# A hybrid attention and recurrence layer: two block sizes per step in the recurrent heads, and four reordered queues

## The chip, the cores and the metric

The kernel runs on one core of a Trainium2 chip. The metric is the device time of one execution in microseconds (us). The core's engines work side by side, each through its own queue of instructions in order: PE (TensorE, matrix products; its weight loads are listed as PEld), DVE (VectorE), ACT (ScalarE), POOL (GpSimd) and SP (SyncE, which issues the DMA transfers). An instruction waits at the head of its queue until what it needs is there, and everything behind it waits too.

## The reference

One decoder layer on 1024 tokens of width 1024, in float32: a normalised input goes through one projection to an attention mixer (8 heads of 64) and to a gated recurrence (4 heads of 128); both results are projected back and added, and a feed-forward block with a squared ReLU follows. For each recurrent head, with f the forget gate of every channel:

```python
def hgrn2_recurrence(q, f_pre, i, gate, lower_bound, out_gain):
    """f = lb + (1-lb) sigmoid(f_pre); S_t = diag(f_t) S_{t-1} + (1-f_t) i_t^T;
    o_t = S_t^T q_t; y = RMSNorm_head(o) * silu(gate)."""
...
    h = rmsnorm(x, mix_pre_norm); proj = h @ w_in
    attn = rmsnorm(dilated_mixture_attention(q_a, k_a, v_a, slopes), attn_out_norm)
    rec = hgrn2_recurrence(q_h, f_h, i_h, g_h, lower_bounds, hgrn_out_norm)
    x = x + rmsnorm(concat([attn, rec]) @ w_out, mix_post_norm)
    ff = square(relu(rmsnorm(x, mlp_pre_norm) @ w_ff1)) @ w_ff2
    x = x + rmsnorm(ff, mlp_post_norm)
```

## The kernel before, in words

**Products.** A large matrix product is made from three products of the high and low parts of its operands (`three_pass`, L86 to L88). `split_into` makes the parts: ACT copies the source, rounded (L82), and VectorE subtracts that from it (L83). In the recurrent heads the products are plain F32. In the feed-forward block the products are recombined in seven per 2x2 blocks (`mm1` for the first matrix, `mm2` for the second).

**Order.** Everything is written out by hand; an engine takes its instructions in the order in which the program issues them. `fill(ns)` takes pieces of projection work off a list of generators until their counted costs (650 for three products of 512 columns, 330 for three of 256) come to `ns`. So the recurrent heads and the attention steps are written with fills between their own steps, and PE has projection products to do while VectorE works. `hgrn_ig` and `hgrn_qf` are such generators (the next head's projections), `attn_proj(pr)` makes an attention pair's queries, values and keys, and `drain` runs what is left.

**Start.** `keep_warm` (L278) issues products of a zero tile. Then the first token block is transposed (`x_turn`), one of eight 128-column pieces at a time, with a warm call between two, and the first weights are split (`w_split`). ACT and VectorE evacuate each transpose.

**A recurrent head.** The decays between a query and an earlier key inside a block of 128 tokens are products over ranges of tokens. `hgrn_core` (L371) builds the 128 x 128 score blocks `at` of the eight token blocks by seven levels, at block sizes c = 1, 2, 4 to 64 (L385). A level multiplies the keys with the second half of the queries of each pair of blocks (L392, eight products of 64 columns into one PSUM bank `pl`), then VectorE multiplies the first halves of the keys (L396) and the second halves of the queries (L398) by the block totals of the decay, makes the totals of twice the size (L402), and copies the level's scores into `at` where a mask says so (L403, a predicated copy). A fill of 2900 follows each level. Ahead of the levels stand a fill of 2200, the diagonal (`pd`, L377, from `prod`, L367), and a fill of 2300. After them `kt` is transposed (`pk`, L414; ACT copies it to `ktr`, L415), and the chunk states (`pu`, L422) and the outputs (`po`, L439, L441) follow. Four heads run one after the other, heads 0 to 2 beside the next head's projections and head 3, whose fills are scaled by 1.15, beside `attn_proj(0)`. The gates of a head are evacuated by `ig_evac`: ACT for the values `inat` (L229), VectorE for `gate` (L230).

**Attention.** 64 steps, each with scores (`ps`), transposes of the weights (`pt`) and sums over values, with fills between; `hooks` runs other work at given steps. `keys_off` (L469, L471) evacuates keys (`kf`, `kh`, `kl`) and copies them by DMA. `v_turn` transposes a pair's values in the middle of a later projection product.

**Output projection.** A loop over the eight token blocks t: `late_out` (products `pwo`), `row_turn` (transposes `pmt`), `residual`, `row_attn` (two VectorE operations that scale a later attention row, L702), `mixed_half`, `next_turn`, `residual_b`.

**Feed-forward.** The opening handles the first two column pairs of the first matrix apart, with the products in the order 1, 2, 3, 5, 6, 4, 7; `out_p5` (L1094), `out_p6` (L1097), `out_p7` and their like evacuate each product, `b_split` and `w1_split` split operands, `w1_load` loads raw pairs. Then `ff1(q)` runs over the other pairs. The second matrix runs over 49 units; behind unit 0 the last pair's activations are summed and stored (`act_sums`, `act_store`). At the end each token block gets its plain part (L1602 adds it), its norm and a gain (L1613).

```python
    for li, c in enumerate(LEVELS):
...
            for n in range(NT):
                TE.matmul(pl[:, n * 64:(n + 1) * 64], kt[:, n * P:(n + 1) * P],
                          qv[:, n * nb:(n + 1) * nb, 1, :], start=True, stop=True)
...
            fill(2900 * scale)
```

Of the kernel before, what the change touches and what calls it, by code (L numbers as in the profile page):

```python
# [17 lines left out]
P = 128  # L18
# [17 lines left out]
def hymba_layer(ctx, tc, x, w_in, w_out, w_ff1, w_ff2, g_pre, lb_logits, g_mix, g_post,  # L36
# [28 lines left out]
    masks = cp.tile([P, len(LEVELS), 64], U8, name="masks")  # L65
    gpre = cp.tile([P, NK], F32, name="gpre")
# [241 lines left out]
    V.tensor_copy(masks, mraw)  # L308
    V.tensor_tensor(out=lb, in0=lbl[:, :, 0], in1=lbl[:, :, 1], op=ALU.subtract)
# [14 lines left out]
    def hgrn_ig(h):  # L324
        hd = heads[h] = new_head(h)
        w_get(4 * h + 1)
        for t2 in range(NT // 2):
# [7 lines left out]
            ig_evac(hd, pm, (t2 * 2, t2 * 2 + 1))  # L335
# [34 lines left out]

    def hgrn_core(h, scale, after=None):  # L371
        hd = heads[h]
        inat, gate, prod, qt, kt, tot = (hd[n] for n in ("inat", "gate", "prod", "qt", "kt", "tot"))
        fill(2200 * scale)
# [8 lines left out]
        cur = tot  # L383
        fill(2300 * scale)
        for li, c in enumerate(LEVELS):  # L385
            nb = 64 // c
            qv = qt.rearrange("p (b two c) -> p b two c", two=2, c=c)
            kv = kt.rearrange("p (b two c) -> p b two c", two=2, c=c)
            av = at.rearrange("p n (b two c) -> p n b two c", two=2, c=c)
            pl = bank("s", f"pl{h}_{li}")  # L390
            for n in range(NT):
                TE.matmul(pl[:, n * 64:(n + 1) * 64], kt[:, n * P:(n + 1) * P],  # L392
                          qv[:, n * nb:(n + 1) * nb, 1, :], start=True, stop=True)
            w = T // (2 * c)
            cv = cur[:, :2 * w].rearrange("p (b two) -> p b two", two=2)
            V.tensor_tensor(out=kv[:, :, 0, :], in0=kv[:, :, 0, :],  # L396
                            in1=cv[:, :, 1:2].to_broadcast([P, w, c]), op=ALU.mult)
            V.tensor_tensor(out=qv[:, :, 1, :], in0=qv[:, :, 1, :],  # L398
                            in1=cv[:, :, 0:1].to_broadcast([P, w, c]), op=ALU.mult)
            nx = slab("P", f"tot{h}_{w}") if w > 64 else \  # L400
# [505 lines left out]
    for t in range(NT):  # L906
# [6 lines left out]
        if t > 0:  # L913
            residual(t - 1)
# [776 lines left out]
```

## Time and profile before

| | us |
|---|---|
| median of three runs (1299.04, 1296.51, 1299.54) | 1299.04 |
| profiled execution | 1296.25 |
| its span | 1294.4 |
| PE busy | 1254.5 (97%) |
| PEld busy | 1071.5 (83%) |
| DVE busy | 857.5 (66%) |
| ACT busy | 515.6 (40%) |
| POOL busy | 295.5 (23%) |

The recurrent heads take the span from about 60 to 320 us, attention goes on to about 600, the output projection to about 700, and the feed-forward block takes the rest. A row of the timeline has the start, the duration, the engine, the line, the operation, the tiles written and read, shapes, the count, and in brackets the idle time of the engine ahead of it and the engine and line that ended it. Successive PE products overlap, so the time that one costs is the distance from start to start and not its duration. The rows that matter stand in the prediction.

### The profile page before, as it was taken

What the parts mean: (1) busy time and instruction counts of PE and PEld (TensorE: products, weight loads), DVE (VectorE), ACT (ScalarE), POOL (GpSimd) and SP (SyncE); (2) the same over time, 40 slices, a digit from 0 to 9 for tenths busy, and PEclk for the clock granted to TensorE, in tenths of its full rate; (3) what the DMA queues carried; (4) which work ended last, traced back from release to release, by engine and by line L of the source; (5) the groups of instructions that cost most, each with busy time, mean ns of one, the idle gap of its engine ahead of it and who ended that gap; (6) DMA issues with size and microseconds to landing.
All of it is one profiled execution on the core that took longest, in us unless ns stands there. A gap on an engine that the chain in (4) does not pass through costs nothing. (4 is left out here: it accounts for less than half of the span.)

```text
span 1294.4 us, 17367 instructions
## 1 busy us (share of the span) xinstructions
PE 1254.5 (97%) x6666; PEld 1071.5 (83%) x6666; DVE 857.5 (66%) x1395; ACT 515.6 (40%) x904; POOL 295.5 (23%) x308
## 2 busy tenths in 40 slices
PE   8999999999999999899999899999999999999997
PEld 8898989988888887787877788888878888888885
DVE  5565656575665656667758566666675777688956
ACT  6612121222555555574655322222234633344412
POOL 0000000011112123134350387575541000000012
PEclk9999999999999999999999999999999999999998
DMA  5201111132223223326242345453478454434423
GB/s 204 66 17 51 33 44 38 29 86 66 82 66 82 66 82 80 127 70 221 97 148 90 138 171 179 147 179 127 142 260 333 163 195 130 156 105 131 156 75 126
DMA packets 58577, 153.98 MB, mean 119 GB/s; under 512 B 4992, under 2 KB 12928, under 8 KB 58240
## 3 DMA queue, kind: packets, MB, share of 16 engines
q1 hardware_dynamic: 58496, 152.89, 35.6%
q8 instruction: 52, 0.85, 0.3%
q14 instruction: 29, 0.24, 0.1%
HBM read 106.73 MB, written 39.85 MB: 113 GB/s over the span
## 5 line engine op out<-in xcount | busy, mean ns | idle before, releaser
L87 PE MATMUL f<-bl,ah 128*128 128x512 f32 x392 | 152.6, 389 | 0.5 <-DVE bl L83 0.5
L86 PE MATMUL f<-bh,ah 128*128 128x512 f32 x392 | 152.6, 389 | 0.0
L88 PE MATMUL f<-bh,al 128*128 128x512 f32 x392 | 152.5, 389 | 0.0
L83 DVE TENSOR_TENSOR al<-ar,ah 128x1024 fp32r<-128x1024 f32 x49 | 60.7, 1239 | 50.2 <-ACT ah L82 21.6
L87 PEld LDWEIGHTS f<-bl,ah 128*128 128x128 f32 x392 | 73.6, 188 | 16.1 <-DVE bl L83 0.8
L86 PEld LDWEIGHTS f<-bh,ah 128*128 128x128 f32 x392 | 73.6, 188 | 15.6 <-ACT acc L1471 0.4
L88 PEld LDWEIGHTS f<-bh,al 128*128 128x128 f32 x392 | 73.6, 188 | 15.1
L82 ACT ACTIVATE ah<-ar 128x1024 fp32r<-128x1024 f32 x49 | 52.3, 1067 | 53.6 <-DMA ar<-actd 28.2
L1607 POOL TENSOR_SCALAR fp<-fss 128x1 f32<-128x1 f32 x8 | 3.5, 432 | 268.3 <-ACT fd L1604 268.3
L576 DVE CUSTOM_DVE_ANT_0 p<-ps,bt 128x512 f32<-128x512 f32 (+2 forms) x84 | 44.3, 552 | 24.1 <-PE ps L574 23.9
L603 ACT ACTIVATE pth<-pt 128x512 fp32r<-128x512 f32 (+2 forms) x96 | 43.2, 486 | 41.1 <-PE pt L600 39.4
L604 DVE TENSOR_TENSOR ptl<-pt,pth 128x512 fp32r<-128x512 f32 (+2 forms) x96 | 50.2, 551 | 13.1 <-ACT pth L603 13.1
L392 PEld LDWEIGHTS pl<-qt,kt 128*128 128x128 f32 x448 | 53.7, 194 | 1.5 <-PE pm_av L88 0.9
L392 PE MATMUL pl<-qt,kt 128*128 128x64 f32 x448 | 53.8, 273 | 0.5 <-DVE qt L398 0.5
L587 ACT ACTIVATE p<-p,nm 128x128 f32<-128x128 f32 (+3 forms) x64 | 49.5, 773 | 9.2 <-DVE nm L582 6.2
L229 ACT ACTIVATE inat<-pig,rstd 128x128 f32<-128x128 f32 x32 | 11.6, 367 | 97.3 <-PE pig L88 84.2
L78 POOL TENSOR_SCALAR ms<-hss 128x8 f32<-128x8 f32 x4 | 0.8, 197 | 210.0 <-DVE hss L444 210.0
L82 ACT ACTIVATE bh<-br 128x1024 fp32r<-128x1024 f32 x28 | 29.9, 1068 | 42.6 <-PE f L88 37.3
L633 POOL TENSOR_TENSOR anat<-anat,rd 128x128 f32<-128x128 f32 x32 | 14.5, 455 | 140.4 <-DVE anat L632 136.6
L600 PE MATMUL pt<-ident,p 128*128 128x128 f32 x288 | 42.9, 276 | 3.4 <-DVE ptl L604 3.4
L1127 POOL TENSOR_TENSOR e<-x,e 128x512 f32<-128x512 f32 x14 | 20.7, 1476 | 102.0 <-DVE x L1078 102.0
L396 DVE TENSOR_TENSOR kt<-kt,tot 128x512 f32<-128x512 f32 x28 | 20.2, 722 | 35.8 <-PE pl L392 35.8
(1586 smaller groups left out, 3869.1 us busy)
## 6 DMA issues: line engine op xcount, KB each, us to landing
ar<-actd SPq DMA_DIRECT2D x49, 512.0 KB, 3.7
raw<-in_w_in_dram SPq DMA_DIRECT2D x28, 512.0 KB, 3.6
w1r<-in_w_ff_dram SPq DMA_DIRECT2D x14, 1024.0 KB, 6.5
br<-in_w_ff_dram SPq DMA_DIRECT2D x14, 1024.0 KB, 6.5
actd<-e SPq DMA_DIRECT2D x17, 768.0 KB, 4.3
actd<-e SPq DMA_DIRECT2D x11, 1024.0 KB, 4.1
xr<-in_x_dram SPq DMA_DIRECT2D x8, 512.0 KB, 8.7
raw<-in_w_out_dram SPq DMA_DIRECT2D x8, 512.0 KB, 3.7
```

The costliest lines, as they stand in the source:

```text
L82: S.activation(hi, src, AF.Copy)
L83: eng.tensor_tensor(out=lo, in0=src, in1=f32(hi), op=ALU.subtract)
L86: TE.matmul(dst, lhs[0], rhs[0], start=start, stop=False)
L87: TE.matmul(dst, lhs[0], rhs[1], start=False, stop=False)
L88: TE.matmul(dst, lhs[1], rhs[0], start=False, stop=stop)
L392: TE.matmul(pl[:, n * 64:(n + 1) * 64], kt[:, n * P:(n + 1) * P], qv[:, n * nb:(n + 1) * nb, 1, :], start=True, stop=True)
L576: V.tensor_tensor_reduce(out=pe[:, k0:k0 + n], in0=pS[:, :n], in1=bts[hd][:, o:o + n], scale=1.0, scalar=-3.0e38, op0=ALU.add, op1=ALU.max ...
L587: S.activation(pe[:, :nk], pe[:, :nk], AF.Exp, bias=nm[:, b:b + 1], accum_out=dn[:, b:b + 1])
L600: TE.transpose(pt[:, j * P:(j + 1) * P], pe[:, jj * P:(jj + 1) * P], ident)
L603: S.activation(hi, src, AF.Copy)
L604: V.tensor_tensor(out=lo, in0=src, in1=f32(hi), op=ALU.subtract)
L1127: eng[0].tensor_tensor(out=e1[:, 3], in0=a21, in1=e1[:, 2], op=ALU.add)
```

## The change

- **Recurrent heads.** The levels at c = 1 to 32 become three steps that each handle two block sizes, c and 2c with c = 1, 4, 16; c = 64 stays a level of its own. `quarter_sets` makes, for each half of the tokens, a set of 192 query columns per token block: the second halves at size c, and the last two quarters of each block of four, without and with the decay of the quarter between. A step makes eight products of 192 columns into four banks (tags s and t), and VectorE then updates queries, keys and totals in quarters and copies each bank into `at` in three predicated copies of 128 elements (12 per step; the third goes by the new masks `near`). The level at c = 64 is copied by ACT without a mask. Fills: 3300 ahead of the diagonal (2200), 1200 (2300), 7000 after each step, 3400 after the last level (2900 after each level).
- The gates of heads 1 to 3 are evacuated by ACT. The masks `near` are made from `masks` at the start.
- **First pair's values.** In `attn_proj(0)` both halves are transposed in the key products, the first in the first, the second in the second; before, the first one in the second value product and the second in the first key product.
- **Four queues.** At the start nine warm calls stand ahead of the transposes, none between, and five behind; the weight splits come earlier. `keys_off` runs behind a step's hooks. `row_attn` runs ahead of `residual`. In the feed-forward opening `out_p6` of each pair follows its part of the T3 split, the splits of pair 2 stand ahead of `out_p3` and `out_p7`, and pair 4 is loaded after them. The stores of the last pair's activations move from unit 0 to unit 2, and at the end the last block's gain is multiplied into both pieces after the second sum.

```diff
...
@@ -279,14 +280,12 @@
      groups = ((0, 1), (1, 1), (2, 2), (4, 2), (6, 1), (7, 1))
-    keep_warm(3)
+    keep_warm(9)
     for k in range(NK):
         x_turn(0, 1, k)
-        keep_warm(1)
-        if k == 3:
+        if k in (3, 4):
             w_split()
-    w_split()
-    keep_warm(2)
+    keep_warm(5)
     for i, grp in enumerate(groups):
         for k in range(NK):
             if i + 1 < len(groups):
@@ -297,8 +296,8 @@
...
         if i == 4:
+            ig_evac(heads[0], pms0[0], PAIRED[0])
             w_split()
-            ig_evac(heads[0], pms0[0], PAIRED[0])
             ig_evac(heads[0], pms0[1], PAIRED[1])
@@ -306,6 +305,11 @@
         ig_evac(heads[0], pms0[q], PAIRED[q])
     w_split()
     V.tensor_copy(masks, mraw)
+    first = col("lowhalf", 3)
+    V.tensor_reduce(first, mraw[:, 0:6].rearrange("p (s two) j -> p s two j", two=2)[:, :, 0], axis=AX.X, op=ALU.max)
+    V.tensor_scalar(first, first, -1.0, 1.0, op0=ALU.mult, op1=ALU.add)
+    V.tensor_tensor(out=near, in0=mraw[:, 0:6].rearrange("p (s two) j -> p s two j", two=2)[:, :, 1],
+                    in1=first.unsqueeze(2).to_broadcast([P, 3, 64]), op=ALU.mult)
...
@@ -332,7 +336,9 @@
                                k == 0, k == NK - 1)
                     if not (u == 1 and k == NK - 1):
                         yield 330.0
-            ig_evac(hd, pm, (t2 * 2, t2 * 2 + 1))
+            for u, t in enumerate((t2 * 2, t2 * 2 + 1)):
+                S.activation(hd["inat"][:, t], pm[:, u, 0], AF.Copy, scale=rstd0[:, t:t + 1])
+                S.activation(hd["gate"][:, t], pm[:, u, 1], AF.Copy, scale=rstd0[:, t:t + 1])
@@ -368,10 +374,35 @@
+    def quarter_sets(hd, h, step, tots):
+
+        c = 4 ** step
+        nb = 32 // c
+        qt = hd["qt"]
+        cv = tots.rearrange("p (n b f) -> p n b f", n=NT, f=4)
+        sets = []
+        for hf in range(2):
+            q = qt[:, hf * 512:hf * 512 + 512]
+            z = slab("T", f"qs{h}_{step}{hf}", F32, (P, 4, 192))
+            n4 = slice(hf * 4, hf * 4 + 4)
+            S.activation(z[:, :, :64].rearrange("p n (g c) -> p n g c", c=c),
+                         q.rearrange("p (n g two c) -> p n g two c", n=4, two=2, c=c)[:, :, :, 1], AF.Copy)
+            z2 = z[:, :, 64:128].rearrange("p n (b two c) -> p n b two c", two=2, c=c)
+            q4 = q.rearrange("p (n b f c) -> p n b f c", n=4, f=4, c=c)
+            S.activation(z2[:, :, :, 0], q4[:, :, :, 2], AF.Copy)
+            V.tensor_tensor(out=z2[:, :, :, 1], in0=q4[:, :, :, 3],
+                            in1=cv[:, n4, :, 2:3].to_broadcast([P, 4, nb, c]), op=ALU.mult)
+            V.tensor_tensor(out=z[:, :, 128:].rearrange("p n (b w) -> p n b w", b=nb),
+                            in0=z[:, :, 64:128].rearrange("p n (b w) -> p n b w", b=nb),
+                            in1=cv[:, n4, :, 1:2].to_broadcast([P, 4, nb, 2 * c]), op=ALU.mult)
+            sets.append(z)
+        return sets, cv
+
     def hgrn_core(h, scale, after=None):
         hd = heads[h]
         inat, gate, prod, qt, kt, tot = (hd[n] for n in ("inat", "gate", "prod", "qt", "kt", "tot"))
-        fill(2200 * scale)
+        ready = quarter_sets(hd, h, 0, tot)
+        fill(3300 * scale)
         pd = bank("t", f"pd{h}")
         for c in range(NT):
             TE.matmul(pd[:, c:c + 1], prod[:, c * P:(c + 1) * P], ones, start=True, stop=True)
@@ -380,32 +411,67 @@
         at = slab("S", f"at{h}", F32, (P, NT, P))
         V.tensor_tensor(out=at, in0=ident.unsqueeze(1).to_broadcast([P, NT, P]),
                         in1=dg.unsqueeze(2).to_broadcast([P, NT, P]), op=ALU.mult)
-        cur = tot
-        fill(2300 * scale)
-        for li, c in enumerate(LEVELS):
...
+        fill(1200 * scale)
+        totals = slab("P", f"tot{h}")
+        for step in range(3):
+            c = 4 ** step
+            nb = 32 // c
+            sets, cv = ready
+            banks4 = []
+            for u in range(4):
+                pl = bank("st"[u // 2], f"pl{h}_{step}{u}").rearrange("p (n q) -> p n q", n=2)
+                for n in range(2 * u, 2 * u + 2):
+                    TE.matmul(pl[:, n % 2, :192], kt[:, n * P:(n + 1) * P], sets[u // 2][:, n % 4],
+                              start=True, stop=True)
+                banks4.append(pl)
+            w = T // (4 * c)
+            at_ = (0, 768, 960)[step]
+            tots = totals[:, at_:at_ + 3 * w].rearrange("p (i w) -> p i w", i=3)
+            u23, u123, nx = (tots[:, i] for i in range(3))
+            cw = cv.rearrange("p n b f -> p (n b) f")
+            q4 = qt.rearrange("p (m f c) -> p m f c", f=4, c=c)
+            k4 = kt.rearrange("p (m f c) -> p m f c", f=4, c=c)
+
+            def spread(ap, k=c):
+                return ap.unsqueeze(2).to_broadcast([P, w, k])
+            V.tensor_tensor(out=q4[:, :, 1], in0=q4[:, :, 1], in1=spread(cw[:, :, 0]), op=ALU.mult)
+            for hf in range(2):
+                n4 = slice(hf * 4, hf * 4 + 4)
+                V.tensor_tensor(out=qt[:, hf * 512:hf * 512 + 512].rearrange("p (n b f c) -> p n b (f c)", n=4, f=4, c=c)
+                                [:, :, :, 2 * c:],
+                                in0=sets[hf][:, :, 128:].rearrange("p n (b w) -> p n b w", b=nb),
+                                in1=cv[:, n4, :, 0:1].to_broadcast([P, 4, nb, 2 * c]), op=ALU.mult)
+            V.tensor_tensor(out=u23, in0=cw[:, :, 2], in1=cw[:, :, 3], op=ALU.mult)
+            V.tensor_tensor(out=u123, in0=cw[:, :, 1], in1=u23, op=ALU.mult)
+            V.tensor_tensor(out=nx, in0=cw[:, :, 0], in1=u123, op=ALU.mult)
+            if step < 2:
+                ready = quarter_sets(hd, h, step + 1, nx)
+            V.tensor_tensor(out=k4[:, :, 2], in0=k4[:, :, 2], in1=spread(cw[:, :, 3]), op=ALU.mult)
+            V.tensor_tensor(out=k4[:, :, 1], in0=k4[:, :, 1], in1=spread(u23), op=ALU.mult)
+            V.tensor_tensor(out=k4[:, :, 0], in0=k4[:, :, 0], in1=spread(u123), op=ALU.mult)
+            for u, pl in enumerate(banks4):
+                for part_, mask, c2 in ((0, masks[:, 2 * step], c), (2, masks[:, 2 * step + 1], 2 * c),
+                                        (1, near[:, step], 2 * c)):
+                    av = at[:, 2 * u:2 * u + 2].rearrange("p n (b two c) -> p n b two c", two=2, c=c2)
+                    V.copy_predicated(
+                        av[:, :, :, 1, :],
+                        mask.rearrange("p (b c) -> p b c", c=c2).unsqueeze(1).to_broadcast([P, 2, 64 // c2, c2]),
+                        pl[:, :, part_ * 64:part_ * 64 + 64].rearrange("p n (b c) -> p n b c", c=c2))
             cur = nx
-            fill(2900 * scale)
+            fill((7000, 7000, 7000)[step] * scale)
+        pl = bank("s", f"pl{h}_6")
+        for n in range(NT):
+            TE.matmul(pl[:64, n * 64:(n + 1) * 64], kt[:, n * P:n * P + 64], qt[:, n * P + 64:(n + 1) * P],
+                      start=True, stop=True)
+        S.activation(at[:64, :, 64:], pl[:64].rearrange("p (n c) -> p n c", n=NT), AF.Copy)
+        kv, qv = (x.rearrange("p (n two c) -> p n two c", two=2, c=64) for x in (kt, qt))
+        cv = cur.rearrange("p (n two) -> p n two", two=2)
+        V.tensor_tensor(out=qv[:, :, 1], in0=qv[:, :, 1], in1=cv[:, :, 0:1].to_broadcast([P, NT, 64]), op=ALU.mult)
+        V.tensor_tensor(out=kv[:, :, 0], in0=kv[:, :, 0], in1=cv[:, :, 1:2].to_broadcast([P, NT, 64]), op=ALU.mult)
+        nx = tp.tile([P, NT], F32, tag="tot8", name=f"tot{h}_8", bufs=1)
+        V.tensor_tensor(out=nx, in0=cv[:, :, 0], in1=cv[:, :, 1], op=ALU.mult)
+        cur = nx
+        fill(3400 * scale)
         ktr = slab("T", f"ktr{h}", F32, (P, NT, P))
         for hf in range(2):
             pt = bank("t", f"pk{h}_{hf}")
@@ -495,7 +561,7 @@
             yield 650.0
         vs = slab("V8", f"v{pr}", F32R, (P, NT, 2, 2, 64))
-        late = None
+        late = []
 
         def v_turn(full, hf):
             pt = bank("mm", f"pvt{pr}{hf}")
@@ -510,13 +576,13 @@
             n = 0
             for cost in proj_t(w, f"av{pr}", hf, box):
                 n += 1
-                if n == 4 and late is not None:
-                    v_turn(*late)
+                if n == 4 and pr > 0 and late:
+                    v_turn(*late.pop(0))
                     cost += 450.0
                 yield cost
             full = half(f"vf{pr}{hf}")
             V.tensor_tensor(out=full, in0=box[0], in1=rrow[:, sl], op=ALU.mult)
-            late = (full, hf)
+            late.append((full, hf))
             yield 650.0
@@ -529,8 +595,8 @@
             n = 0
             for cost in proj_t(w, f"ak{pr}", hf, box):
                 n += 1
-                if n == 3 and hf == 0:
-                    v_turn(*late)
+                if n == 3 and late:
+                    v_turn(*late.pop(0))
                     cost += 450.0
                 yield cost
@@ -872,9 +938,6 @@
         if not fresh:
             look(s + 2)
         turn(hd, b, exped.pop(s))
-        if b in (7, 0, 1):
-            while put_off:
-                keys_off(*put_off.pop())
         if b % 2:
             to_weigh.append((hd, b // 2))
         to_fold, last_fold = [(i, g, weigh(i, g)) for i, g in ready], to_fold
@@ -888,6 +951,9 @@
         for i, g, a in last_fold:
             finish(i, g, *a)
         hooks.get(s, lambda: None)()
+        if b in (7, 0, 1):
+            while put_off:
+                keys_off(*put_off.pop())
         fill(3400.0 - 360.0 * b if s < n_steps - 20 else 1000.0 if s < n_steps - 16 else 1300.0)
         finish(i, g, *a)
@@ -910,10 +976,10 @@
             if t + 4 < NT:
                 row_load(t + 4)
+        if NE <= t + 2 < NT:
+            row_attn(t + 2)
         if t > 0:
             residual(t - 1)
-        if NE <= t + 2 < NT:
-            row_attn(t + 2)
...
@@ -1298,23 +1364,28 @@
     for q in range(2):
         mm1(q, 6, "b", True)
         w1_drop(q, "S")
-    b_split("T3", h11)
+    b_open("T3")
+    for c in range(2):
+        split_into(bops["T3"][2 * c], bops["T3"][2 * c + 1], h11[:, 2 * c:2 * c + 2])
+        out_p6(c)
     large.add("A")
-    for q in range(2):
-        out_p6(q)
     w1_sums(2, V)
     for q in range(2):
         mm1(q, 4, "d", False)
     wide_split(2)
+    wd = large.get("wd2", F32R)
+    split_into(wd[:, 0:2], wd[:, 2:4], w1raw[2][:, 2:4])
+    ops1[2]["D"] = wd
+    ops1[2][7], ops1[2][4] = halves_of((wd[:, 0:2], wd[:, 2:4]))
+    drop(w1raw.pop(2))
+    w1_load(4)
+    w1_split(2, 3)
     for q in range(2):
         out_p3(q)
     for q in range(2):
         mm1(q, 7, "b", False)
         w1_drop(q, "D")
         out_p7(q)
-    w1_split(2, 2)
-    w1_load(4)
-    w1_split(2, 3)
     act_plain(0)
     act_plain(1)
 
@@ -1573,6 +1644,7 @@
         drop(*aop.pop(n), *bop.pop(n))
         if n == 0:
             act_sums(NPAIR - 1)
+        if n == 2:
             act_store(NPAIR - 1)
         if h == nh - 1:
             for i in range(4):
@@ -1609,8 +1681,9 @@
                     end_out(*late)
                 if t < 2:
                     fold_in(7, 5, t)
-            if last:
-                V.tensor_tensor(out=c, in0=c, in1=gend[:, j], op=ALU.mult)
+            if last and j:
+                for i, e in enumerate(pieces):
+                    V.tensor_tensor(out=e, in0=e, in1=gend[:, i], op=ALU.mult)
...
```

More of the change, by code (lines that the diff above doesn't have):

```diff
@@ L382, in hgrn_core @@
                         in1=dg.unsqueeze(2).to_broadcast([P, NT, P]), op=ALU.mult)
-        cur = tot
-        fill(2300 * scale)
-        for li, c in enumerate(LEVELS):
[L386 to L400, printed above, removed]
-                tp.tile([P, w], F32, tag=f"tot{w}", name=f"tot{h}_{w}", bufs=1)
-            V.tensor_tensor(out=nx[:, :w], in0=cv[:, :, 0], in1=cv[:, :, 1], op=ALU.mult)
-            V.copy_predicated(
-                av[:, :, :, 1, :],
-                masks[:, li].rearrange("p (b c) -> p b c", c=c).unsqueeze(1).to_broadcast([P, NT, nb, c]),
-                pl.rearrange("p (n b c) -> p n b c", n=NT, c=c))
-            cur = nx
-            fill(2900 * scale)
```

5 lines of the change are left out of this document (3 added, 2 removed).

## The prediction

> **What bounds the kernel now.** I read the page first (PE 97% busy), then busy times by stretch, then what PE waited for, and only then the timelines of the places that the change touches.
>
> ```profile
> 60.00:265.00 205.00, 203.03 (x1432) 189.57 (x1431) 123.38 (x228) 40.78 (x70) 5.50 (x6) 0.99 0.14 43
> ...
> 735.00:1280.00 545.00, 543.85 (x2396) 449.11 (x2396) 385.82 (x409) 186.06 (x229) 165.28 (x123) 1.00 0.47 163
> ```
>
> Columns: stretch, its length, then PE, PEld, DVE, ACT, POOL busy, PE clock, DMA. In the three recurrent heads that overlap the projections (60 to 265 us) PE is busy for 203.0 of 205.0 us and DVE for 123.4. From 735 us on PE never rests either. So a microsecond of PE work or PE waiting that goes before 735 us reaches the end nearly whole, and VectorE has some 80 us to spare in the heads, if its work comes at the right moments.
>
> **Part 1, PE in the heads.** Now seven levels with eight products of 64 columns; then three steps with eight products of 192 columns, and eight of 64. A plain F32 product is two instructions.
>
> ```profile
> 10.46 1.46 PE L278 MATMUL pig<-warm 128*128 128x256 f32 x6
> ...
> 11.75 0.27 PE L254 MATMUL xt<-ident,xr 128*128 128x128 f32 x1
> ...
> 97.22 1.90 PE L392 MATMUL pl<-qt,kt 128*128 128x64 f32 x16
> 98.92 0.36 PE L86 MATMUL pig<-wig1h,hTh 128*128 128x256 f32 x1
> 99.12 0.28 PE L87 MATMUL pig<-wig1l,hTh 128*128 128x256 f32 x1
> 99.24 0.28 PE L88 MATMUL pig<-wig1h,hTl 128*128 128x256 f32 x1
> ...
> 111.42 1.72 PE L422 MATMUL pu<-inat,ktr 128*128 128x128 f32 x14
> 112.90 0.48 PE L86 MATMUL pm_q<-hTh,wh 128*128 128x512 f32 x1
> ```
>
> From start to start: 64 columns 0.106 us ((98.92-97.22)/16), 128 columns 0.106 (1.48/14), 256 columns 0.215 (1.29/6). A product of 64 columns thus costs as much as one of 128, and 192, halfway between 128 and 256, should take 0.160. The first product after a group takes 0.20 instead of 0.12: 0.08 for each change. Per head now 7 x (1.70+0.08) = 12.5 us; then 3 x (16 x 0.160 + 0.08) + 1.78 = 9.7. Four heads: -11.0 us. Bounds by the rows on either side: at 0.106 it would be -21.4, at 0.215 -0.6.
>
> **Does VectorE keep up?** Its added work must lie under the fill of PE work between steps.
>
> ```profile
> 75.63 0.68 DVE L402 TENSOR_TENSOR tot<-tot 128x512 f32<-128x512 f32 x1
> 76.23 1.32 DVE L403 COPY_PREDICATED at<-masks,pl 128x512 f32<-128x512 uint8 x1
> 77.34 0.33 DVE L230 TENSOR_SCALAR gate<-pig,rstd 128x128 f32<-128x128 f32 x1
> ...
> 80.65 0.42 DVE L402 TENSOR_TENSOR tot<-tot 128x256 f32<-128x256 f32 x1
> 80.98 1.32 DVE L403 COPY_PREDICATED at<-masks,pl 128x512 f32<-128x512 uint8 x1
> ...
> 85.67 0.28 DVE L402 TENSOR_TENSOR tot<-tot 128x128 f32<-128x128 f32 x1
> 85.87 0.70 DVE L403 COPY_PREDICATED at<-masks,pl 128x512 f32<-128x512 uint8 x1
> ```
>
> Back to back a product of 512 elements costs 0.60, of 256 0.33, of 128 0.20. The predicated copy costs 1.11 at blocks of one and two, 0.70 from four on; in quarters (128 elements) I take 0.33 and 0.20, between 0.16 (a quarter of the short one) and 0.70 (a fixed price). Step 0 in order: three qt products 0.99, three totals 0.99, the sets of step 1 on VectorE 2 x (0.20+0.33) = 1.06, three kt products 0.99, twelve copies 4.0: 8.0 us. Steps 1 and 2: 5.9 and 4.6. A step's period on PE is 2.6 us of products and 7000 of fill, which is 21 products of three (330 counted, 0.36 long: 0.12 each above), 7.6 us: 10.2. The tighter loop is that next products need the four banks free, so kt products and copies (1.0+4.0) must end within 7.6. Both hold; PE doesn't wait. The gate evacuation of heads 1 to 3 goes to ACT (eight of 0.33 off VectorE per head), which is busy for 41 of 205 us and takes the copies of the sets too. If that cover were gone, each microsecond over 10.2 per step would cost twelve. PE's order, longer fills included, leaves queued projection work until the end of heads 0 to 2, so nothing is exposed there.
>
> ```profile
> PE pd L377 <- DVE prod L367: 2.0, 2, 1.0
> ```
>
> The row has the total, the times and the longest. The fill ahead of `pd` grows from 2200 to 3300: some 1.2 us more of PE work, over the longest wait of 1.0: -2.0.
>
> ```profile
> 137.50:140.90 3.40, 3.40 (x18) 3.40 (x18) 0.79 (x1) 0.00 (x0) 0.00 (x0) 0.50 0.54 154
> ...
> 728.00:731.40 3.40, 3.40 (x10) 2.62 (x9) 0.29 (x1) 0.00 (x0) 0.00 (x0) 0.50 0.19 69
> ```
>
> Right after one of these waits PE's granted clock is 0.50 for 3.4 us, a loss of 1.7. With the wait gone I count -1.2 (seven chances in ten that it goes). The Trainium skill (TensorE: Matmul & The Clock Gate, Part 1) has the clock halved after an idle window of about 3.4 us; the first of these dips follows a wait of one microsecond only, so the row decides, and I keep the three chances.
>
> **Head 3.** Its fills at 1.15 times run through attn_proj(0), 48 products of 650 and two of 450. The new sum up to `ktr`, 33,200, uses up all 32,100; now 28,500 are used and 3,600 still cover `ktr`.
>
> ```profile
> 273.89 1.54 DVE L396 TENSOR_TENSOR kt<-kt,tot 128x512 f32<-128x512 f32 x1 [1.04 <-PE pl L392]
> ```
> ```profile
> 309.51 1.28 ACT L471 ACTIVATE kh<-kf 64x512 fp32r<-64x512 f32 x2 [5.83 <-DVE kf L469]
> 310.83 1.09 ACT L415 ACTIVATE ktr<-pk 128x512 f32<-128x512 f32 x2
> ```
>
> Then `ktr` stands bare behind two key copies on ACT: 0.7 for kf, 1.3, and half of 1.1, less the transposes: +1.9. Products that meet POOL's subtractions take 1.54 instead of 0.69, so the first step there may run over: +0.5; a wait of 0.5 on qt goes. Together +1.9. The values' transpose one product later (v_turn) is the same work, under the same products: nothing; without that cover it would show as a wait on `vf` of at most one product's 0.6.
>
> **Part 2, the ff1 opening.**
>
> ```profile
> 711.52 0.47 PE L1059 MATMUL f10b<-T30h,wd0h 128*128 128x512 f32 x1 [1.37 <-DVE x L1097]
> ...
> 722.87 1.04 ACT L82 ACTIVATE wd2h<-w1r 128x1024 fp32r<-128x1024 f32 x1
> ...
> 726.51 0.47 PE L1059 MATMUL f12d<-T40h,wd2h 128*128 128x512 f32 x1 [3.84 <-DVE x L1094]
> ```
>
> out_p6(0) no longer stands behind the second T3 split (1.13): product 7 starts 1.2 earlier, at 710.3. The wd2 and wf splits now precede twelve ACT and VectorE evacuations, instead of waiting on ACT until 722.87. VectorE then finishes out_p7 by 721.1, out_p5(2) by 721.7, and f12d starts at 721.9: -4.6, with 0.5 still waiting on L1094, the next late one. The clock dip at 728 follows this wait: -1.7. The load of pair 4 now waits for the slot of w1r2 (some 6 us later, needed 20 us after): nothing; were it late, 0.2 per microsecond at most shows, since POOL reads it first.
>
> **Part 3, the other queues.**
>
> ```profile
> 2.26 2.93 PE L278 MATMUL pig<-warm 128*128 128x256 f32 x6 [2.26 <-ACT warm L204]
> ...
> 7.68 0.66 PE L278 MATMUL pig<-warm 128*128 128x256 f32 x2
> ...
> 10.92 1.05 ACT L82 ACTIVATE wig0h<-raw 128x1024 fp32r<-128x1024 f32 x1
> ...
> 12.06 0.37 ACT L255 ACTIVATE hTh<-xt,gpre 128x128 fp32r<-128x128 f32 x1
> ...
> 13.29 0.38 PE L87 MATMUL pig<-wig0l,hTh 128*128 128x256 f32 x1 [0.87 <-DVE wig0l L83]
> ```
>
> Start: nine warm calls (18 instructions) now stand ahead of the first transpose. At 0.45 apiece until about 7.7, where the pairs get short, and 0.215 after, they end at 9.0. Then four evacuations and a split on ACT, one and a split, and the subtraction, 0.37, 1.05 and 1.2 each: about 14.4 instead of 13.29, +1.1. By the Trainium skill (the same section) the clock opens after some 3.4 us of work, whatever its count: eight cold, ten fast, an estimated end at 7.8 and a total 1.2 us lower; the row at 7.68 shows it two microseconds later, and I keep the row. The masks' three operations lie under projections.
>
> ```profile
> 515.03 1.28 ACT L471 ACTIVATE kh<-kf 64x512 fp32r<-64x512 f32 x2 [1.53 <-DVE kf L469]
> 516.34 0.60 ACT L82 ACTIVATE emt<-pmt 128x512 fp32r<-128x512 f32 x1
> ```
>
> keys_off behind the hooks: `emt` and the w_out split go 1.8 earlier on ACT, and the next exponential and transposes then stand behind kh, some 1.4 later; SP issues the weight load ahead of the four key copies. 0, between -2 and +2; elsewhere (no hook at that step) it is nothing.
>
> ```profile
> 601.09 0.63 PE L718 MATMUL pmt<-ident,row 128*128 128x128 f32 x4 [1.49 <-DVE row L702]
> ...
> 605.75 0.50 PE L86 MATMUL pwo<-wh,mt 128*128 128x512 f32 x1 [0.40 <-ACT mt L82]
> ```
>
> row_attn ahead of residual takes this 1.49 away, but lengthens by its own 0.73 the chain residual, x2r, residual_b, mixed_half, mt on which PE waits 4.7 us later. What PE gains at 601 it waits for at 605: +0.7 (from -1.5 to +1).
>
> ```profile
> 997.20 0.50 PE L87 MATMUL f<-bl,ah 128*128 128x512 f32 x1 [0.47 <-DVE bl L83]
> ```
> ```profile
> 1286.05 0.68 DVE L1613 TENSOR_TENSOR acc<-acc,gend 128x512 f32<-128x512 f32 x1
> 1286.65 0.68 DVE L1602 TENSOR_TENSOR acc<-fe,acc 128x512 f32<-128x512 f32 x1
> ```
>
> The stores of act_sums no longer stand on SP ahead of the loads behind the wait at 997: -0.5. At the end the add needn't wait for the first gain product: -0.6.
>
> **Sum**, in us: -11.0 -2.0 -1.2 +1.9 -4.6 -1.7 +1.1 +0.7 -0.5 -0.6 = -17.9. The profiled execution took 1296.25 (span 1294.4 and 1.85 around it), which gives 1278.4; the median of the runs is 2.79 above it, which gives 1281.1. I take 1279.5.
>
> **Rivals.** (a) VectorE does not keep up in step 0: if each instruction costs its duration instead of its pitch (0.28 for 128 elements, 0.42 for 256) and writes in blocks of one cost double as in L403, step 0 takes 11.8 us against 10.2: 1.6 x 4, and some 2 more in head 3 beside POOL: 1288. For it: L403 at 1.32. Against it: L402 at 512 elements, blocks of one, costs 0.60.
> (b) The wide products gain nothing: at 0.215 each the head's PE work is that of now, and 10.4 of the 11.0 are gone: 1290. For it: no row has 192 columns. Against it: 128 and 256 differ just by their columns.
> (c) Slower: a predicated copy has a fixed price. At 0.70 for 128 elements the loop from one step's products to the next is 1.0+12 x 0.70+0.2 = 9.6 against 7.6: 2.0 x 12 = 24 us, and 1303. It begins to bind at 0.53 and outweighs the rest at 0.66. Against it: the same instruction takes 1.11 and 0.70 at the same size, so it goes by elements.
>
> **Chances.** My forecast 0.62 (its own range 1270 to 1287), (a) 0.16, (b) 0.10, (c) 0.12. A measurement of this kernel tells about 0.3%, 3.9 us, from no change: faster 0.83, within it 0.05 (the far side of (a) and (b) together), slower 0.12. The range 1269 to 1294 takes in (a), (b) and the bounds of the small terms, and leaves out (c).
>
> **What will show it.** Products of 192 columns 0.16 apart, 2.6 us a group; no PE wait on L377's prod; no PE wait above 0.6 on DVE in the heads except at the end of head 3; step 0's quarter copies at 0.33, the later ones at 0.20; f12d without its 3.8; the first main product near 14.4; a wait at `pwo` in place of `pmt`. It is wrong if PE waits in every step for a bank that a copy holds, or if new clock dips come elsewhere.

## The result and the profile after

The changed kernel takes 1298.08 us (median of 12 runs), the kernel before 1297.56 in the same 12 rounds: a ratio of 1.0001, 95% interval 0.9992 to 1.001. Nothing can be told from no change, where 1279.5 was forecast. The profiled execution has a span of 1295.2 (before: 1294.4).

The stretch view of the changed kernel, with the columns as in the prediction:

```profile
60.00:265.00 205.00, 200.47 (x1325) 182.19 (x1325) 151.45 (x363) 62.04 (x140) 6.04 (x6) 1.00 0.14 44
265.00:320.00 55.00, 46.25 (x223) 38.41 (x222) 39.33 (x94) 12.29 (x23) 10.82 (x8) 0.91 0.24 63
```

PE is no longer covered in the heads: 4.5 us idle in the first stretch, 8.75 in head 3, where the granted clock also falls to 0.91. What PE waits for (total, times, longest):

```profile
PE pm_ak L87 <- DVE vf L584: 5.0, 1, 5.0
...
PE pl L424 <- DVE at L456: 3.8, 11, 0.6
...
PE f12d L1127 <- DVE ws L84: 2.5, 1, 2.5
PE po L505 <- DVE st L494: 2.5, 3, 1.1
...
PE f12d L1125 <- DVE x L1160: 2.1, 1, 2.1
PE ph L871 <- DVE esum L861: 1.9, 1, 1.9
PE pu L488 <- ACT ktr L481: 1.9, 1, 1.9
PE pwo L87 <- DVE ad L848: 1.5, 1, 1.5
```

Gone are the waits of `pd` (2.0) and of `pmt` on `row` (1.5), and the 3.84 of `f12d` on L1094 (now L1160) is down to 2.08. The others of these rows are new or longer, and all but the one on `ktr` are waits for VectorE. Cutting both traces at the first product of each stage shows where the time went. A stage's time is the start of the next one less its own start.

| From the first ... to the first ... | before | after | difference | forecast |
|---|---|---|---|---|
| span's start to `pl` | 72.48 | 72.06 | -0.4 | +1.1 |
| `pl` to `pm_aq` (heads 0 to 2) | 192.20 | 185.59 | -6.6 | -11.5 |
| `pm_aq` to `po` of head 3 | 52.39 | 61.14 | +8.8 | -0.9 |
| that `po` to `pwo` (attention) | 260.30 | 260.19 | -0.1 | 0 |
| `pwo` to `f10a` (output projection) | 78.65 | 81.25 | +2.6 | +0.7 |
| `f10d` to `f12c` (opening) | 41.07 | 39.37 | -1.7 | -6.3 |
| `f115a` to `fe` (last pair, second matrix) | 287.80 | 286.87 | -0.9 | -0.5 |
| last product to the span's end | 8.80 | 8.10 | -0.7 | -0.6 |

In the last column the -11.0 is spread over the four heads, and -2.0 and -1.2 stand with heads 0 to 2. The stages left out are equal within 0.05. Three rows carry the miss: head 3 (9.7 us), heads 0 to 2 (4.9), and the opening (4.6). The output projection adds 1.9.

**Heads 0 to 2: PE's side came as forecast, and better.** The timeline of PE in head 0:

```profile
72.06 2.77 PE L424 MATMUL pl<-qs,kt 128*128 128x192 f32 x16
74.53 0.41 PE L87 MATMUL pig<-wig1h,hTh 128*128 128x256 f32 x1
...
103.63 1.15 PE L464 MATMUL pl<-qt,kt 128*64 128x64 f32 x16
104.70 0.50 PE L87 MATMUL pm_q<-hTh,wh 128*128 128x512 f32 x1
```

Sixteen instructions of 192 columns take 2.47 us from start to start, 0.154 each (0.160 forecast). The level at 64 takes 1.07 (1.78 forecast, with 0.08 for the change of group): it now loads 64 of the 128 columns of each key block (`128*64` in its row). VectorE's side did not:

```profile
73.55 0.62 DVE L437 TENSOR_TENSOR qt<-qt,tot 128x256 f32<-128x256 f32 x1
...
74.75 0.62 DVE L444 TENSOR_TENSOR tot<-tot 128x256 f32<-128x256 f32 x1
75.41 0.62 DVE L445 TENSOR_TENSOR tot<-tot,tot 128x256 f32<-128x256 f32 x1
...
78.19 0.63 DVE L449 TENSOR_TENSOR kt<-kt,tot 128x256 f32<-128x256 f32 x1
...
79.81 0.44 DVE L456 COPY_PREDICATED at<-masks,pl 128x128 f32<-128x128 uint8 x1
...
84.48 0.44 DVE L456 COPY_PREDICATED at<-near,pl 128x128 f32<-128x128 uint8 x1
84.73 0.44 DVE L437 TENSOR_TENSOR qt<-qt,tot 128x256 f32<-128x256 f32 x1
...
88.12 0.42 DVE L449 TENSOR_TENSOR kt<-kt,tot 128x256 f32<-128x256 f32 x1
```

The first step takes VectorE from 73.55 (L437) to 84.73, 11.2 us, where 8.0 was forecast and PE comes back after 10.2. At blocks of one an operation on 256 elements costs 0.53 to 0.66 from start to start (at blocks of four, L449, 0.34), and twelve copies 4.92, 0.41 each instead of 0.33. So the thirteen operations ahead of the copies take 6.26 (4.0 in the forecast), and the copies 4.92 (4.0).

**Head 3** goes wrong on VectorE's queue. VectorE and one row of POOL, then the PE row that waits:

```profile
268.27 3.25 POOL L558 TENSOR_TENSOR ql<-qf,q 64x512 fp32r<-64x512 f32 x2 [12.92 <-ACT q L557]
268.65 1.70 DVE L444 TENSOR_TENSOR tot<-tot 128x256 f32<-128x256 f32 x1
270.39 1.53 DVE L445 TENSOR_TENSOR tot<-tot,tot 128x256 f32<-128x256 f32 x1
...
283.63 2.04 DVE L84 TENSOR_TENSOR wl<-raw,wh 128x1024 fp32r<-128x1024 f32 x1 [2.44 <-ACT wh L83]
285.59 0.41 DVE L437 TENSOR_TENSOR qt<-qt,tot 128x256 f32<-128x256 f32 x1
...
293.38 1.28 DVE L584 TENSOR_TENSOR vf<-pm_av,rrow 128x512 f32<-128x512 f32 x2
```
```profile
288.83 0.39 PE L89 MATMUL pm_av<-hTh,wl 128*128 128x512 f32 x1
294.21 0.77 PE L87 MATMUL pm_ak<-hTh,wh 128*128 128x512 f32 x1 [4.99 <-DVE vf L584]
```

The evacuations `vf` of both value halves stand behind the whole second step (285.6 to 293.4), and the key product needs the PSUM bank that the first of them frees. The step itself is late, because beside POOL's subtractions L444 and L445 take 1.70 and 1.53 instead of 0.62, and the weight split 2.04 instead of 1.22. From the end of that wait on, and again behind the one on `ktr`, PE runs at a granted clock of 0.51 and 0.50:

```profile
292.20:299.00 6.80, 4.79 (x14) 4.54 (x15) 4.95 (x14) 0.00 (x0) 0.00 (x0) 0.51 0.25 78
316.00:319.40 3.40, 3.15 (x16) 2.85 (x15) 1.86 (x6) 0.00 (x0) 0.90 (x1) 0.50 0.72 148
```

### The profile page after: what moved, and what is told of

Read it like the earlier page. It is cut to its first block, busy times and chain, and to the rows that moved or that the text cites. A ratio compares the mean times of both kernels' runs of the same rounds, so it can differ in the third digit from the quotient of the medians.

```text
span 1295.2 us, 17262 instructions
## 1 busy us (share of the span) xinstructions
PE 1245.5 (96%) x6476; PEld 1057.5 (82%) x6476; DVE 895.3 (69%) x1574; ACT 537.3 (41%) x980; POOL 298.2 (23%) x308
## 5 line engine op out<-in xcount | busy, mean ns | idle before, releaser
L84 DVE TENSOR_TENSOR wl<-raw,wh 128x1024 fp32r<-128x1024 f32 x23 | 31.4, 1364 | 18.2 <-ACT wh L83 17.8
L424 PE MATMUL pl<-qs,kt 128*128 128x192 f32 x192 | 37.9, 343 | 3.9 <-DVE at L456 3.8
L666 PEld LDWEIGHTS pt<-ident,p 128*128 128x128 f32 x288 | 33.5, 141 | 9.4 <-DVE ptl L670 6.8
L683 PE MATMUL pov<-pth,v 128*128 128x256 f32 (+1 forms) x160 | 40.5, 288 | 0.0
```

The source lines that it names most:

```text
L84: eng.tensor_tensor(out=lo, in0=src, in1=f32(hi), op=ALU.subtract)
L424: TE.matmul(pl[:, n % 2, :192], kt[:, n * P:(n + 1) * P], sets[u // 2][:, n % 4], start=True, stop=True)
L666: TE.transpose(pt[:, j * P:(j + 1) * P], pe[:, jj * P:(jj + 1) * P], ident)
L683: TE.matmul(po[:, c0:256], vst, pt[j // 4][q][:, j % 4, c0:], start=j == 0 and q == 0, stop=j == nj - 1 and q == 1)
```

## The experiments

All ratios are against the kernel before on the same chip.

### Which half of the change costs what

Edit 1: the changed heads with all queues as before. Edit 2: the old heads with all reordered queues. Edit 3: the changed kernel, with the old levels in head 3 only:

```diff
 def hgrn_core(h, scale, after=None):
+    old = h == HH - 1
+    if not old:
         ready = quarter_sets(hd, h, 0, tot)
-    fill(3300 * scale)
+    fill((2200 if old else 3300) * scale)
...
+    if old:
+        # fill(2300 * scale), the seven levels with fill(2900 * scale) behind each
+    else:
         # the three steps and the level at 64
```

> Only the change in the recurrent heads (steps of two block sizes, gates on ACT, the first pair's values later); the queues as before. Theory H (head 3 eats the gain): head 3's first step products start some 6.6 us earlier than before (271.96), its outputs po some 2 us later than before (317.07), and nothing changes behind them: about 1299.5, +2 against before. Rival Q (the heads gain as forecast and the reordered queues give it back): about 1289, -8.

Measured 1297.2, ratio 1.0001 (0.999 to 1.0012).

> The old heads with all reordered queues (start, keys_off, row_attn, feed-forward opening, stores, last gain). Theory H: the queues together are worth about -1.5 (start -0.4, keys_off -0.4, row_attn +2.6, opening -1.7, stores and tail -1.6): about 1296. Rival Q: +8, about 1306.

Measured 1297.8, ratio 1.0004 (0.9993 to 1.0014).

> The changed kernel with the seven old levels and their fills in head 3 alone; the values' transposes stay in the key products. Theory H: no PE wait of 5 us on vf, no clock of 0.5 in head 3, po of head 3 near 310 instead of 318.79: -8.8, about 1289. Rival V (the later transposes of the values hold the PSUM bank and cause the wait): the wait on vf stays, and the time is that of the changed kernel, about 1298.

Measured 1288.76, ratio 0.9943 (0.9923 to 0.9963).

Neither half moves the time, so rival Q falls. The two totals that theory H named are not shown either: +2 for the heads alone can't be told from nothing, and the -1.5 of the queues alone lies just outside the interval (-0.9 to +1.8). In the trace of edit 2 the clock falls to 0.50 twice after the waits of `pd` (0.89 and 0.97), where the kernel before has one such fall, and heads 0 to 2 take 193.50 against 192.20. The place of the loss is told, though: with edit 1 the stretch from `pm_aq` to `po` takes 61.29, with edit 3 53.19, and the gain of heads 0 to 2 stays (185.63 and 185.68). Head 3 ate what heads 0 to 2 gained: with the old levels there, the time is some 7 to 8 us below that of the kernel before. With edit 3 the values are still transposed in the key products and there is no wait on `vf`, so rival V falls as the cause.

### The opening: POOL beside VectorE

```diff
 if nq:
+    if nq == 3:
+        held = tp.tile([P, 1], F32, tag="held", name="held", bufs=1)
+        G.tensor_copy(held, f32(ops1[2]["D"][:, 3, 511:]))
     w1_sums(nq)
```

> The changed kernel with one small POOL copy of the last column of the wd2 low part ahead of POOL's sums for pair 3, so that these start behind VectorE's splits. Theory P (POOL's and VectorE's operations on SBUF slow each other): L1082 and L1083 take 0.69 instead of 1.81 and 1.78, the ws and wd subtractions 1.22 instead of 2.29 and 2.31; the waits of f12d (2.55 and 2.08) fall to about 0.5 together: -4, about 1294. Rival O (the order of the splits on VectorE alone makes f12d wait): the waits stay, about 1298.

Measured 1294.16, ratio 0.9977 (0.9967 to 0.9986). VectorE and POOL in the changed kernel, then with the edit:

```profile
717.44 1.29 POOL L1080 TENSOR_TENSOR ss<-w1r 128x512 f32<-128x512 f32 x1 [33.29 <-DVE ss L1081]
...
717.48 1.81 DVE L1082 TENSOR_TENSOR s<-w1r,ss 128x512 f32<-128x512 f32 x1
719.21 1.78 DVE L1083 TENSOR_TENSOR w1r<-w1r 128x512 f32<-128x512 f32 x1
720.91 2.29 DVE L84 TENSOR_TENSOR ws<-ss,ws 128x1024 fp32r<-128x1024 f32 x1
722.08 2.27 POOL L1083 TENSOR_TENSOR w1r<-w1r 128x512 f32<-128x512 f32 x1
723.12 2.31 DVE L84 TENSOR_TENSOR wd<-w1r,wd 128x1024 fp32r<-128x1024 f32 x1
```
```profile
717.62 0.69 DVE L1082 TENSOR_TENSOR s<-w1r,ss 128x512 f32<-128x512 f32 x1
718.23 0.68 DVE L1083 TENSOR_TENSOR w1r<-w1r 128x512 f32<-128x512 f32 x1
718.84 1.22 DVE L84 TENSOR_TENSOR ws<-ss,ws 128x1024 fp32r<-128x1024 f32 x1
720.10 1.23 DVE L84 TENSOR_TENSOR wd<-w1r,wd 128x1024 fp32r<-128x1024 f32 x1
...
721.93 1.30 POOL L1080 TENSOR_TENSOR ss<-w1r 128x512 f32<-128x512 f32 x1
```

The same four operations in the same order lose 4.4 us when POOL's four sums for pair 3 run beside them, and nothing when these start behind them. PE's waits at `f12d` fall from 2.55 and 2.08 to 0.7 in all, so rival O falls. The stage goes from 39.37 to 35.12, against 41.07 before: -6.0, where the prediction had -6.3. So the reordering was worth what was forecast, and meeting POOL's sums took most of it back. The Trainium skill (SBUF — State Buffer, section "SBUF: two separate sides") has a VectorE operation with two SBUF inputs and a POOL operation that reads SBUF take a shared pair of ports in turn, each for its whole length. The rows agree: each of the four is longer by 1.1, and a POOL sum takes 1.30 alone and up to 2.27 beside them.

### Head 3: order or neighbour

Edit 5 puts part of the fill ahead of the second step's VectorE work; edit 6 holds POOL's first query subtraction until the step's key products are done.

```diff
 # 5: behind the products of a step
+early = 2600.0 if h == HH - 1 and step == 1 else 0.0
+if early:
+    fill(early)
...
-fill((7000, 7000, 7000)[step] * scale)
+fill((7000, 7000, 7000)[step] * scale - early)
 # 6: ahead of the copies of a step; low() is POOL's subtraction and its two DMAs
+while lows:
+    G.tensor_copy(col("hold"), kt[:, T - P:T - P + 1])
+    lows.pop(0)()
```

> The changed kernel; in head 3, 2600 counted ns of the fill behind the second step's products are taken ahead of that step's VectorE work, so that the first evacuation of the values stands ahead of the step's 24 VectorE operations instead of behind them. PE's order stays. Theory D (VectorE's order): the wait of 4.99 on vf goes, but VectorE ends the step no earlier (294 us), so the third step's products wait for the copies instead, 3 to 4 us in small pieces: -1 to -3, about 1296. Rival S (only this evacuation was in the way): -5 and -1.7 for the clock, about 1291.

Measured 1295.28, ratio 0.9979 (0.9969 to 0.9988).

> The changed kernel; in head 3, POOL's subtractions for the first half of the queries are held by a small copy that needs the step's key products, so that they run beside VectorE's copies out of PSUM and not beside its operations on SBUF. Theory P (POOL and VectorE slow each other on SBUF): L444 and L445 take 0.62 each instead of 1.70 and 1.53, the first step's copies end 2 us earlier, PE's waits for them fall from 1.6 to about 0.5, the wait on vf from 5.0 to about 4: -2, about 1296. Rival N (VectorE's order alone makes head 3 late): nothing changes, 1298.

Measured 1294.83, ratio 0.998 (0.9971 to 0.999). PE with edit 5, VectorE and POOL with edit 6:

```profile
291.90 4.73 PE L424 MATMUL pl<-qs,kt 128*128 128x192 f32 x16 [1.74 <-DVE at L459]
```
```profile
269.98 0.60 DVE L445 TENSOR_TENSOR tot<-tot 128x256 f32<-128x256 f32 x1
270.62 0.62 DVE L446 TENSOR_TENSOR tot<-tot,tot 128x256 f32<-128x256 f32 x1
```
```profile
275.22 2.64 POOL L565 TENSOR_TENSOR ql<-qf,q 64x512 fp32r<-64x512 f32 x2
```
```profile
275.87 0.45 DVE L460 COPY_PREDICATED at<-near,pl 128x128 f32<-128x128 uint8 x1
```

Both theories hold, each for a part. With edit 5 the wait on `vf` is gone and the third step's products wait for the copies instead, 1.74 in one piece where 3 to 4 in small pieces were expected; the stage takes 58.16 instead of 61.14, so rival S, which had some 7 us, falls. With edit 6 the totals take 0.60 and 0.62, and PE's waits for the first step's copies fall from 1.6 to 0.34; the stage takes 59.15, so rival N falls. The copies that POOL now runs beside read PSUM and keep their 0.45 (0.44 without POOL). One expectation missed: the wait on `vf` stays 4.99, since PE came 2 us earlier as well.

### The fills of heads 0 to 2, and row_attn

```diff
-fill((7000, 7000, 7000)[step] * scale)
+fill(((8000, 7000, 6000) if h < HH - 1 else (7000, 7000, 7000))[step] * scale)
...
-fill(3000 * scale)   # ahead of pu
+fill((1700 if h < 2 else 3000) * scale)
...
-fill(2600 * scale)   # behind pu
+fill((3900 if h < 2 else 2600) * scale)
...
-if NE <= t + 2 < NT:
-    row_attn(t + 2)
 if t > 0:
     residual(t - 1)
+if NE <= t + 2 < NT:
+    row_attn(t + 2)
```

> The changed kernel with two edits at different places. Heads 0 to 2: fills of 8000, 7000, 6000 behind the steps instead of 7000 each, and in heads 0 and 1 the fill ahead of pu 1700 instead of 3000 and the one behind it 3900 instead of 2600, so that the weight split stands behind the state chain on VectorE. Output projection: row_attn behind residual again. If the waits of PE in these heads are VectorE's lateness at just these points: the seven waits for copies (2.2 in all) fall under 0.4 and the two waits of po (1.13 each) go: -4. The old order of row_attn: the waits of 1.90 and 1.50 go, the one of 1.49 on row comes back: -2. Together about 1292. If the waits only move on, 1296 or more.

Measured 1289.74, ratio 0.9934 (0.9919 to 0.995). Heads 0 to 2 in the changed kernel, then with the edit:

```profile
72.06:257.65 185.59, 181.05 (x1204) 164.69 (x1203) 136.54 (x334) 53.86 (x124) 6.04 (x6) 1.00 0.12 38
```
```profile
73.17:252.95 179.78, 179.15 (x1205) 164.91 (x1203) 136.14 (x334) 53.81 (x124) 6.04 (x6) 1.00 0.13 39
```

PE's idle time falls from 4.5 to 0.6 and its busy time by 1.9: -5.8, and -12.4 against before, where -11.5 was forecast. (A stop costs busy time as well: in head 3 of the changed kernel a group that stops for each of its banks shows four pieces of 0.89, 3.56 in all, and the group at 72.06, which doesn't stop, 2.77.) The waits were VectorE's lateness at two points: the first step, and a weight split of 2.36 (two subtractions). VectorE's rows of the changed kernel show it directly ahead of the state chain; in the kernel before, and with the edit, it stands behind it.

```profile
114.39 2.36 DVE L84 TENSOR_TENSOR wig2l<-raw,wig2h 128x1024 fp32r<-128x1024 f32 x2 [0.26 <-ACT wig2h L83]
116.66 0.29 DVE L492 COPY st<-pu 128x128 f32<-128x128 f32 x1
```

In the output projection the stage goes back from 81.25 to 78.74. There the moved row_attn stood beside POOL's own row product (598.37 to 599.66, and 633.05 to 634.32) and took longer:

```profile
598.35 1.72 DVE L768 SCALAR_TENSOR_TENSOR row<-row,ara,gmix 128x384 f32<-128x384 f32 x1
...
633.24 1.50 DVE L768 SCALAR_TENSOR_TENSOR row<-row,ara,gmix 128x384 f32<-128x384 f32 x1
```
```profile
600.33 0.61 DVE L702 SCALAR_TENSOR_TENSOR row<-row,ara,gmix 128x384 f32<-128x384 f32 x1
```

The first pair is the changed kernel, the last row the kernel before; with edit 7 it takes 0.61 again. Edit 7 shows that the order costs the 2.5 us; how much of that is POOL isn't shown apart, since no run holds POOL here.

### All together, and head 3 once more

Edit 8 is edits 3, 4 and 7 at once. Edit 9 is edits 4 and 7 with the new steps in head 3 too, with edits 5 and 6 and the values' weight split ahead of the second query evacuation:

```diff
 yield from proj_t(w, f"aq{pr}", hf, box)
+if pr == 0 and hf == 1:
+    w_get(A0 + 1)
```

> All edits that should help at once: old levels in head 3, the fills of heads 0 to 2 and the old row_attn order as in the run before, POOL's sums for pair 3 held. If the pieces are independent: -8.8 -4 -4 -2 from the changed kernel, about 1279. If the clock dips come back at new waits, 1.7 more for each.

Measured 1276.81, ratio 0.9845 (0.9828 to 0.9861): 1.55% faster than before, and faster than the changed kernel.

> The combined kernel (fills of heads 0 to 2, old row_attn order, POOL's sums for pair 3 held), but with the new steps in head 3 too and VectorE's order mended there: POOL's first query subtraction held, the weight split of the values ahead of the second query evacuation, 2600 of the fill ahead of the second step's VectorE work. If VectorE's order and POOL's neighbourhood are the whole trouble of head 3: no wait on vf, no wait above 0.5 before ktr, from the first query product to po about 51 instead of 61.1 (53.2 with the old levels): about 1275. If head 3 simply has too little PE work to cover VectorE, 55 or more, and about 1279.

Measured 1281.11, ratio 0.9879 (0.9863 to 0.9894). PE in head 3 with edit 9:

```profile
285.44 3.45 PE L425 MATMUL pl<-qs,kt 128*128 128x192 f32 x16 [1.89 <-DVE at L463]
...
296.23 0.50 PE L87 MATMUL pm_ak<-hTh,wh 128*128 128x512 f32 x1 [2.08 <-DVE v L589]
```

The stage takes 56.06, not 51: the second of the two expected outcomes. 4.3 us of waits for copies and evacuations are left, and 1.90 on `ktr`, so in this form the old levels (53.16 with edit 8) are better there. That head 3 has too little PE work to cover VectorE fits this but isn't shown: in this trace VectorE also stood idle for 3.4 us ahead of `vf`, which waited for a half-width buffer that POOL's second subtraction held, and whether another buffer would close the gap wasn't tried.

### The values' transposes

```diff
-if n == 4 and pr > 0 and late:
+if n == 4 and late:
```

Edit 10 puts this into edit 9, edit 11 into the changed kernel.

> The run before it, with the first pair's values transposed as before the change (the first half in the second value product, the second half in the first key product). The prediction's step says nothing changes. By VectorE's order the transposes need the first evacuation of the values already in the second value product, which here is early enough: within 1 us of the run before it.

Measured 1283.03, ratio 0.9889 (0.9872 to 0.9906).

> The changed kernel with the values' transposes alone put back. The prediction's step says nothing changes: 1298. By VectorE's order the transposes of the first half stand behind the fourth product of the second value half, near 285 us, and need the evacuation that ends at 294 us: the wait becomes one of 8 to 9 at pvt instead of 5 at pm_ak, 3 to 4 us more, about 1301.

Measured 1300.16, ratio 1.0025 (1.0012 to 1.0039). PE with edit 10, then with edit 11:

```profile
287.98 0.80 PE L87 MATMUL pm_ak<-hTh,wh 128*128 128x512 f32 x1 [4.95 <-DVE v L589]
```
```profile
294.45 1.12 PE L569 MATMUL pvt<-ident,vf 128*128 128x128 f32 x4 [7.60 <-DVE vf L584]
```

Put back alone, the transposes wait 7.6 us for the same late evacuation, and the kernel is some 2 to 3 us slower than the changed one (its stage takes 63.53 instead of 61.14): doing them later was not free of effect but a remedy. Edit 10's expectation of no difference missed in the trace (a wait of 4.95 in place of the two of edit 9, and the stage 59.36 instead of 56.06); the two total times can't be told apart. Most of the difference of the two stages is the clock: PE's waits in head 3 come to 7.7 and 7.1 us, but in edit 10 the granted clock is 0.50 behind the long wait (288 to 292 us) and again at the end of the stage, and in edit 9 it stays at 1.00.

## Why the prediction was wrong

- **PE in the heads (-11.0):** right. With the waits gone (edit 7) heads 0 to 2 gain 12.4 against 11.5 forecast (8.3 of products and the 3.2 of the next point). The width of 192 columns was sized to 4%, the level at 64 was sized too high by 0.7 per head.
- **The waits on `prod` and the clock dip behind one (-3.2):** right. Both are gone.
- **"Both hold; PE doesn't wait" (VectorE keeps up under the fill):** this step failed. The first step was summed at 8.0 us, and VectorE took 11.2. The durations came from rows whose operands lie side by side or in pairs, and one element of four costs 0.53 to 0.66 per 256 elements, not 0.33. Rival (a) was right that VectorE doesn't keep up in the first step, at half its price: PE waited 2.2 in heads 0 to 2 and 1.6 in head 3, bank by bank. That its 11.8 comes so near is partly luck: its durations give 5.2 for the thirteen operations and leave 6.6 for the copies, and they took 6.3 and 4.9. Of the signs of being wrong that the prediction named, the bank waits came behind the first step alone, and the new clock dips came. The weight split that now stands ahead of the state chain (2.26 in two waits) was not looked for at all.
- **Head 3 (+1.9):** the step that cost most. Only what stands bare behind the fills was priced (the wait on `ktr`, which came at 1.90). That evacuations of the filler stand in VectorE's queue behind a whole step, and that one PSUM bank ties PE to them, was left out: 4.99 of waiting, 1.6 at the first step, and two clock dips, which cost half of PE's busy time in them (2.4 and 1.6). "The values' transpose one product later: nothing" was wrong too: put back alone it costs 2 to 3 us (edit 11). And the wait on `vf`, bounded there at 0.6, was 4.99, at the bank and not at the transposes.
- **The opening (-4.6 -1.7):** the mechanism was right, and edit 4 shows 6.0 of the 6.3. Left out was that VectorE's operations then run beside POOL's sums, at 1.1 for each of four.
- **row_attn (+0.7):** right in sign and in the new waits (`pwo` 0.80); the size was 2.6, since the chain waits twice more (1.90 and 1.50), where the moved operations also meet POOL.
- **keys_off (0), stores (-0.5), the end (-0.6):** right, with -0.1, -0.9 and -0.7. **Start (+1.1):** not seen; -0.4 lies within what the start moves between runs of the new start (the product of the row at 13.29 starts at 12.80 to 14.28 in them). The first transpose, behind the eighteen warm instructions, starts at 7.8 here and between 7.7 and 9.2 in those runs; the sum had 9.0.

That the sum came out at nothing was no single rival. Rival (a) covers about 4 us of the miss. POOL beside VectorE in head 3 was priced (0.5 in the sum, 2 in rival (a)), in the opening it was not; and what cost most in head 3, the evacuations behind a step in VectorE's queue, stood in none.

## What to carry to other kernels

When VectorE's work per step grows, the question isn't whether the step ends within PE's fill, but what else the fill itself puts into VectorE's queue behind the step, and which bank or split PE waits for there. Before moving VectorE's work in time, look at what POOL does at the new place: two operations on SBUF side by side cost up to 1.1 us each here, one that reads PSUM nothing. When several stages share an edit, give each its own version: here three heads gained 6.6 us (12.4 with fitted fills) from an edit that cost the fourth 8.8.

## What the runs showed of the hardware

- VectorE and POOL slow each other by 0.5 to 1.1 us for each operation on SBUF (0.61 to 1.13 and 1.72, 0.69 to 1.81, 1.22 to 2.29 on VectorE; 1.30 to 2.27 on POOL), and not where VectorE reads PSUM (0.44 and 0.45).
- One element of four costs VectorE 0.62 for 256 elements; four neighbours of sixteen 0.42.
- A product of 64 columns with 64 of 128 weight columns takes 0.067 per instruction from start to start (1.07 for sixteen), with all 128 it takes 0.106.
- The granted clock falls to 0.50 at some waits and not at others: at 4.99 (for 6.8 us) and 1.90 (for 3.4 us) in head 3 of the changed kernel, not at its 2.55 at `f12d`; at both waits of about 1.0 on `prod` with edit 2, at one of the two before. The Trainium skill (TensorE: Matmul & The Clock Gate, Part 1) has PE's activity watched in windows that run freely, so that one kernel meets them at different points from run to run. That agrees with the run of edit 3, where the same wait of 2.55 has a granted clock of 0.67 behind it from 716 to 720 us; no run here shows the windows themselves.
